# Low parts of the weight blocks by a negated rounding on ScalarE and an accumulating DMA

## Chip, core and metric

The kernel runs on one core of a Trainium2 chip. The metric is the device time of one execution in microseconds (us); the kernel before has a median of 1077.81 us in three runs (1077.65 to 1078.84).

## What is computed

One step of a two-layer decoder trunk, for 1024 prompt tokens and 8 x 4 sample tokens (1056 columns in all, model width 1024), in float32:

```python
# layer 0 (RG-LRU)
u = rmsnorm(x) @ w_in                 # 1024 -> 2 x 1536
xc = causal_conv(u[:1536]);  h = lru_scan(gates(xc), xc)
x = x + (h * silu(u[1536:])) @ w_out
# layer 1 (HGRN2, 8 heads of 128)
q, f, v, gate = split(rmsnorm(x) @ w_in, 4)
o, S = gated_linear_recurrence(silu(q), k(f), v, log_g(f), S0)
x = x + (norm(o) * silu(gate)) @ w_out
y = rmsnorm(x)
```

The outputs are y and the new states of both layers.

## The kernel before

**Split operands.** TensorE multiplies rounded float32 (fp32r). For full precision every operand is held as two blocks, hi = round(x) and lo = x - hi, and a product is three matmuls per 128x128 block (mm3, L241 to L243): hi x hi, hi x lo, lo x hi. For a weight block of 128 partitions and up to 512 columns the steps are these: SP issues the load into a raw buffer (L308), ScalarE rounds raw into hi (L376, L656, L1423, L1648), and GpSimd subtracts, lo = raw - hi (through subtract, L321, or directly, L657 and L1649). In the first 40 us VectorE does some of these subtractions. There are three raw buffers and four slots each for hi and lo in rings (L335); a slot is written again when the matmuls that read it are done. GpSimd also splits activations and does other small work.

**Stages.** Layer 0 runs the input projection (project0, by_chunk) in blocks of 128 outputs over three chunks of 352 columns, with the recurrence (lru) beside it, in four groups; the output projection of three groups is out (residual x loaded from DRAM, added on VectorE at L632 or L696, stored again; nine x buffers, L625), and out_last does the rest with the weights of `load` kept in free tiles. Layer 1 takes its first two heads (HC = 2) with plain products through weights, and the other six with half-size products: seven (L1396) makes two output blocks from seven products of half size instead of eight, after Strassen and Winograd. There split (L1421) rounds and subtracts a raw block or a sum of raw blocks, and combine (L1429) makes those sums on GpSimd, writing over the raw buffers. Five raw buffers serve it; a call of seven has 7 splits and 4 combines, and there are two calls for each of six heads. Between the products lie four bursts per head (burst1 to burst4) with the recurrence: small matmuls on PE and a chain on VectorE (own_gate L1061, scale L1031 and L1040, evacuations L1504 and L1519). The sums of activations that the half-size products read (build, parted_sum: L1363, L321) are made while the first two heads run. Last comes the output projection in two parts; the weights of the second are the eight blocks of `late` (L1640 to L1650).

**Order.** Nothing runs in the order of the program text. Each operation is given to Flow (L39) with its engine, an estimated time, what it reads and writes, a priority and, for a DMA, its size. plan and back (L100, L138) schedule forward and backward several times; each engine then gets its instructions in the order of the best plan. The products of the main chain keep their order on PE. For layer 0 a random search (L165, 3000 tries) also moves operations of the first 60 us. An estimate that changes anywhere can thus change the order everywhere. The warm-up matmuls (L726, 48 calls) fill PE at the start.

The helper that the change adds has these estimates: an activation counts 0.25 + 0.0007 n us on ScalarE, a GpSimd operation with two inputs 0.1 + 0.00245 n, and the new DMA issue 0.93 on GpSimd, with n / 2 KB to move.

Of the kernel before, what the change touches and what calls it, by code (L numbers as in the profile page):

```python
# [14 lines left out]
F32 = mybir.dt.float32  # L15
# [3 lines left out]
AF = mybir.ActivationFunctionType  # L19
ALU = mybir.AluOpType  # L20
# [189 lines left out]
def tile_trunk(ctx: ExitStack, tc: tile.TileContext, xT, prm, hc, w0, wg, wo0, w1, wo1, s_in,  # L210
# [83 lines left out]
    with ExitStack() as l0:  # L294
# [12 lines left out]
        def dma(dst, src, r=(), w=(), prio=5, kb=180, q=Q):  # L307
            fl.add("SP" if q is Q else "ACT", 0.45, lambda: q.dma_start(dst, src), r, w, prio, kb * (1.0 if r else 0.75))  # L308

        def act(n, emit, r, w, prio=5, more=0.0):  # L310
            fl.add("ACT", 0.25 + 0.0007 * n + more, emit, r, w, prio)
# [4 lines left out]
        def pool(n, emit, r, w, prio=5):  # L316
            fl.add("POOL", 0.1 + 0.00245 * n, emit, r, w, prio)
# [45 lines left out]

        def weights(src, n, prio=2, e=G, at=None, q=Q, own=()):

            own = iter(own)
            got = []
            for a in range(0, n, 512):
                m = min(512, n - a)
                raw, *rk = next(own, None) or next(raws)  # L370
                if at:
                    (hi, hk), (lo, lk) = ((o[:, a:a + m], k) for o, k in at)
                else:
                    (hi, hk), (lo, lk) = next(his), next(los)
                dma(raw[:, :m], src[:, a:a + m], (), rk, prio, m / 2, q)
                act(m, lambda hi=hi, raw=raw, m=m: S.copy(hi[:, :m], raw[:, :m]), rk, (hk,), prio)  # L376
                subtract(e, m, lo[:, :m], raw[:, :m], hi[:, :m], (*rk, hk), (lk,), prio)
                got.append((hi, lo, hk, lk))
# [267 lines left out]
        def out_last(src):  # L646
# [3 lines left out]
            def load(m, k, n, hi, hks, lo, lks, kept=()):  # L650
# [5 lines left out]
                act(u, lambda: S.copy(hi, raw[:, :u]), (rk,), (*hks, a), 1)  # L656
                pool(u, lambda: G.tensor_tensor(lo, raw[:, :u], hi.bitcast(F32), op=ALU.subtract), (rk, a), (*lks, b), 1)  # L657
                for i in range(n):
# [266 lines left out]
    with ExitStack() as l1:  # L925
# [470 lines left out]
        def seven(h, a, b, order, at=()):  # L1396
# [24 lines left out]
            def split(p):  # L1421
                (raw, rk), (hi, hk), (lo, lk) = slot[named[p]], next(his), next(los)
                act(512, lambda: S.copy(hi, raw), (rk,), (hk,), 2)  # L1423
                subtract(G, 512, lo, raw, hi, (rk, hk), (lk,), 2)
                parts[p] = hi, lo, (hk, lk)
# [215 lines left out]
        for m in range(KD):  # L1641
# [6 lines left out]
            act(nl, lambda hi=hi, raw=raw: S.copy(hi, raw[:, :nl]), (rk,), (hk,), 1)  # L1648
            pool(nl, lambda hi=hi, lo=lo, raw=raw: G.tensor_tensor(lo, raw[:, :nl], hi.bitcast(F32), op=ALU.subtract), (rk, hk), (lk,), 1)  # L1649
            late.append((hi, lo, (hk, lk)))  # L1650
# [165 lines left out]
```

## Time and profile before

| | |
|---|---|
| median of three runs | 1077.81 us |
| the profiled execution | 1075.47 us |
| its span, first to last instruction | 1073.7 us |
| mean granted TensorE clock | 0.996 |
| instructions on DVE, ACT, POOL | 1535, 1395, 546 |
| DMA issued by SP | 98.67 MB, 28.1% of 16 engines' span |
| DMA issued by GpSimd | none |

PE is TensorE's matmuls, PEld its weight loads, DVE VectorE, ACT ScalarE, POOL GpSimd, and SP issues most DMAs. Lines are those of the kernel before. A group's row has line, engine, operation, out<-in by the program's names, shapes and count, then busy us and mean ns of one, then the engine's idle time before it and what ended it. A row of waits has engine and line of what waited, what it waited for, then the total in us, the number of times and the longest. A row of a timeline has start, length, and the instruction. The page's row of a DMA issue has the name of the tile, count, KB each and the median us from issue to landing. wlo and whi are the low and rounded parts of weights.

### The profile page before, as it was taken

To read this page: it belongs to the slowest core of one execution; us is meant where nothing else is said; L and a number is where in the kernel's file an instruction comes from. 1 tells how busy PE (TensorE), PEld (TensorE's weight loads), DVE (VectorE), ACT (ScalarE), POOL (GpSimd) and SP (SyncE) were. 2 spreads that over 40 slices of the span, in tenths; PEclk is the share of its full clock that TensorE was granted. 3 is DMA by queue.
4 is the path that set the end of the run, shared out by engine and by line. 5 is a ranking of instruction groups with operands and counts; after the bars stand their busy time and mean duration, and the time that the engine had idled before them with its cause. 6 is when DMAs were issued, how large, how long until landed. Compare 5 with 4: busy or idle time off the path is not lost.

```text
span 1073.7 us, 25345 instructions
## 1 busy us (share of the span) xinstructions
PE 1053.0 (98%) x9972; PEld 1024.5 (95%) x9972; DVE 808.2 (75%) x1535; ACT 611.1 (57%) x1395; POOL 558.0 (52%) x546
## 2 busy tenths in 40 slices
PE   9999999999999999999999998999999999999997
PEld 9999999999999999999998997999999999989996
DVE  8999996887997787283999997767768585774446
ACT  7578656867665964243364563747474655752323
POOL 3425353353543547455574854656566665541545
PEclk9999999999999999999999999999999999999998
DMA  9101112124832775240110121212121212354204
GB/s 302 59 27 43 56 49 71 58 61 126 271 104 66 222 252 176 103 131 34 60 51 24 49 92 43 100 43 91 35 92 41 91 44 80 116 169 160 85 1 162
DMA packets 70119, 103.05 MB, mean 96 GB/s; under 512 B 9200, under 2 KB 51184, under 8 KB 70000
## 3 DMA queue, kind: packets, MB, share of 16 engines
q1 hardware_dynamic: 67696, 98.67, 28.1%
q10 hardware_dynamic: 2304, 2.77, 0.8%
q8 instruction: 78, 1.28, 0.5%
q14 instruction: 41, 0.34, 0.1%
HBM read 71.05 MB, written 25.49 MB: 90 GB/s over the span
## 4 chain that ended last, share of the span: by engine, by line
PE 82%; DVE 14%; issue 1%; DMA 1%; ACT 1%; POOL 0%; SPq 0%; POOLq 0%; ACTq 0%; DVEq 0%
PE mm L241 23%; PE mm L242 22%; PE mm L243 22%; PE hg L1049 2%; DVE R L1363 1%; DVE R L1031 1%; PE hg L1266 1%; PE hg L565 1%; DVE tmp L1363 1%; PE hg L1158 1%; DVE a L1232 1%; PE hg L1268 1%; DVE sg L1031 1%; PE hg L241 1%; PE hg L242 1%
## 5 line engine op out<-in xcount | busy, mean ns | idle before, releaser
L241 PE MATMUL mm<-xh,whi 128*128 128x352 f32 (+1 forms) x1143 | 359.3, 314 | 7.2 <-DVE sg L1504 4.5
L242 PE MATMUL mm<-xl,whi 128*128 128x352 f32 (+1 forms) x1143 | 353.2, 309 | 0.0
L243 PE MATMUL mm<-xh,wlo 128*128 128x352 f32 (+1 forms) x1143 | 353.2, 309 | 0.0
L321 POOL TENSOR_TENSOR wlo<-wraw,whi 128x512 fp32r<-128x512 f32 (+2 forms) x131 | 175.9, 1351 | 168.7 <-ACT whi L376 83.6
L241 PEld LDWEIGHTS mm<-xh,whi 128*128 128x128 f32 x1143 | 214.7, 188 | 10.5 <-DVE sg L1504 6.0
L242 PEld LDWEIGHTS mm<-xl,whi 128*128 128x128 f32 x1143 | 215.0, 188 | 1.6 <-DVE xl L321 0.2
L243 PEld LDWEIGHTS mm<-xh,wlo 128*128 128x128 f32 x1143 | 214.9, 188 | 0.0
L497 DVE SCALAR_TENSOR_TENSOR k<-xb,prm_sb,k 128x352 f32<-128x352 f32 (+2 forms) x144 | 90.1, 637 | 10.9 <-ACT k L494 6.1
L241 PE MATMUL mm<-t,whi 128*128 128x264 f32 (+1 forms) x306 | 89.5, 293 | 0.0
L242 PE MATMUL mm<-t,whi 128*128 128x264 f32 (+1 forms) x306 | 87.7, 287 | 0.0
L243 PE MATMUL mm<-t,wlo 128*128 128x264 f32 (+1 forms) x306 | 87.5, 286 | 0.0
L580 POOL TENSOR_TENSOR k<-X 128x352 f32<-128x352 f32 x36 | 44.9, 1256 | 47.8 <-DVE R L581 38.6
L321 POOL TENSOR_TENSOR wlo<-R,whi 128x512 fp32r<-128x512 f32 x33 | 49.9, 1511 | 32.8 <-ACT whi L1423 28.9
L376 ACT CAST whi<-wraw 128x512 fp32r<-128x512 f32 (+2 forms) x83 | 46.0, 574 | 28.5 <-PE mm L242 16.9
L241 PEld LDWEIGHTS mm<-t,whi 128*128 128x128 f32 x306 | 57.6, 188 | 0.7 <-ACT k L1481 0.5
L1504 DVE TENSOR_TENSOR k<-mm,k 128x264 f32<-128x264 f32 x62 | 26.5, 430 | 41.5 <-PE mm L243 41.4
L243 PEld LDWEIGHTS mm<-t,wlo 128*128 128x128 f32 x306 | 57.7, 188 | 0.0
L242 PEld LDWEIGHTS mm<-t,whi 128*128 128x128 f32 x306 | 57.6, 188 | 0.0
L1031 DVE TENSOR_TENSOR R<-R,sg 128x512 f32<-128x512 f32 (+1 forms) x48 | 50.4, 1050 | 0.1
L241 PE MATMUL mm<-yh,whi 128*128 128x352 f32 x153 | 49.9, 326 | 0.0
L243 PE MATMUL mm<-yh,wlo 128*128 128x352 f32 x153 | 49.4, 323 | 0.0
L242 PE MATMUL mm<-yl,whi 128*128 128x352 f32 x153 | 49.4, 323 | 0.0
(415 smaller groups left out, 2684.6 us busy)
## 6 DMA issues: line engine op xcount, KB each, us to landing
wraw<-in_w_dram SPq DMA_DIRECT2D x91, 256.0 KB, 2.6
wraw<-in_wo_dram SPq DMA_DIRECT2D x34, 192.0 KB, 2.5
si<-in_s_in_dram SPq DMA_DIRECT2D x8, 512.0 KB, 4.2
out_ss_out_dram<-si SPq DMA_DIRECT2D x8, 512.0 KB, 2.6
sg<-x1b SPq DMA_DIRECT2D x21, 176.0 KB, 2.8
x<-sg SPq DMA_DIRECT2D x21, 176.0 KB, 1.8
R<-in_w_dram SPq DMA_DIRECT2D x14, 256.0 KB, 2.5
R<-td SPq DMA_DIRECT2D x72, 44.0 KB, 2.0
```

The costliest lines, as they stand in the source:

```text
L241: T.matmul(out, wh, xh, start=first, stop=False, skip_group_check=chained)
L242: T.matmul(out, wh, xl, start=False, stop=False, skip_group_check=chained)
L243: T.matmul(out, wl, xh, start=False, stop=last, skip_group_check=chained)
L321: emit = lambda: e.tensor_tensor(b, x, a.bitcast(F32), op=ALU.subtract)
L376: act(m, lambda hi=hi, raw=raw, m=m: S.copy(hi[:, :m], raw[:, :m]), rk, (hk,), prio)
L497: dve(u, lambda src=src, dst=dst, sh=sh, k=k: V.scalar_tensor_tensor(dst, sh(src, k), pc("cw", 12 * k + m), dst, op0=ALU.mult, op1=ALU.add ...
L565: fl.add("PE", 0.62, lambda ps=ps, i=i, c=c: T.matmul(ps[:96, :CH], gs[:, i, :], ST[:96, chunk(c)], start=True, stop=True), (("gs",), *((" ...
L580: pool(CH, lambda x=x, a=a, b=b: G.tensor_tensor(x, a.bitcast(F32), b.bitcast(F32), op=ALU.add), (ak, bk), (xk,), 3)
L1031: dve(n // 2, lambda sv=sv, dv=dv, s=s, f=f: V.tensor_tensor(dv[:, :, s, :], sv[:, :, s, :], f, op=ALU.mult), (*sk, *gk), dk if i == o els ...
L1049: T.matmul(ps[32 * j:32 * j + 32, n * w:n * w + w], B[:, o:o + 32], q(slice(o, o + 32)), start=True, stop=True, tile_position=(0, 32 * j))
L1363: dve(n, lambda: V.tensor_tensor(o, a, b, op=op), r, (w,), prio, True)
L1504: dve(QT, lambda: V.tensor_tensor(o[0], z[0], u[0], op=ALU.add), (z[1], u[1]), (o[1],), 0)
```

## The change

A new helper `low` makes the low part without hi: ScalarE writes -round(raw) into lo, and a DMA issued by GpSimd adds raw to it (an accumulating DMA). So lo = raw - round(raw) as before. It is used for every weight block that GpSimd subtracted through weights (the default e=G becomes e=None), for the blocks of split in seven, and for the eight late blocks: 176 blocks by the counts of the code. The 18 blocks of `load` in out_last go from GpSimd to VectorE. Blocks for which the call names an engine (the first six of layer 0), the gate weights of lru, and all activations stay. The DMA reads raw and reads and writes lo, so combine and the next load into that raw buffer wait for its landing. The added lines shift later line numbers by 5 to 8.

```diff
+        def low(n, dst, src, r, w, prio=5):
+
+            act(n, lambda: S.activation(dst, src, AF.Copy, scale=-1.0), r, w, prio)
+            fl.add("POOL", 0.93, lambda: G.dma_start(dst.bitcast(F32), src, accum_op=ALU.add), (*r, *w), w, prio, n / 2)
+
...
-        def weights(src, n, prio=2, e=G, at=None, q=Q, own=()):
+        def weights(src, n, prio=2, e=None, at=None, q=Q, own=()):
...
-                subtract(e, m, lo[:, :m], raw[:, :m], hi[:, :m], (*rk, hk), (lk,), prio)
+                if e is None:
+                    low(m, lo[:, :m], raw[:, :m], rk, (lk,), prio)
+                else:
+                    subtract(e, m, lo[:, :m], raw[:, :m], hi[:, :m], (*rk, hk), (lk,), prio)
...
-                pool(u, lambda: G.tensor_tensor(lo, raw[:, :u], hi.bitcast(F32), op=ALU.subtract), (rk, a), (*lks, b), 1)
+                subtract(V, u, lo, raw[:, :u], hi, (rk, a), (*lks, b), 1)
...
-                subtract(G, 512, lo, raw, hi, (rk, hk), (lk,), 2)
+                low(512, lo, raw, (rk,), (lk,), 2)
...
-            pool(nl, lambda hi=hi, lo=lo, raw=raw: G.tensor_tensor(lo, raw[:, :nl], hi.bitcast(F32), op=ALU.subtract), (rk, hk), (lk,), 1)
+            low(nl, lo, raw[:, :nl], (rk,), (lk,), 1)
```

## Prediction

> **What bounds the kernel now.** I read the page first: busy time, then the engines of the chain that ended last.
>
> ```profile
> span 1073.7 us, 25345 instructions
> ...
> PE 1053.0 (98%) x9972; PEld 1024.5 (95%) x9972; DVE 808.2 (75%) x1535; ACT 611.1 (57%) x1395; POOL 558.0 (52%) x546
> ...
> PE 82%; DVE 14%; issue 1%; DMA 1%; ACT 1%; POOL 0%; SPq 0%; POOLq 0%; ACTq 0%; DVEq 0%
> ```
>
> TensorE is idle for 1073.7 - 1053.0 = 20.7 us, and the change leaves every matmul as it is. So it can gain 20.7 us at most, whatever it takes off GpSimd. Next, a table by stage says where the idle time lies, and the view of waits of PE says for whom.
>
> ```profile
> 0.00:50.00 50.00, 47.83 (x317) 46.73 (x318) 44.56 (x99) 32.27 (x67) 18.63 (x27) 1.00 0.58 193
> 50.00:500.00 450.00, 450.00 (x2770) 443.32 (x2769) 353.85 (x632) 286.04 (x561) 208.97 (x234) 1.00 0.35 109
> ...
> 565.00:570.00 5.00, 2.98 (x82) 2.60 (x81) 4.93 (x5) 3.86 (x9) 3.75 (x3) 1.00 0.07 16
> ...
> 645.00:655.00 10.00, 6.12 (x55) 5.24 (x55) 9.72 (x19) 1.99 (x4) 5.12 (x6) 1.00 0.03 9
> ...
> 660.00:935.00 275.00, 271.89 (x3880) 262.08 (x3881) 189.93 (x376) 165.41 (x438) 171.66 (x139) 1.00 0.21 72
> ...
> 1050.00:1073.70 23.70, 16.94 (x127) 15.68 (x125) 14.33 (x35) 7.97 (x18) 11.74 (x14) 0.83 0.52 184
> ```
>
> ```profile
> PE mm L241 <- DVE sg L1504: 4.5, 7, 0.8
> PE mm L241 <- DVE attns L1056: 2.7, 1, 2.7
> PE hg L1049 <- DVE R L1061: 2.0, 1, 2.0
> PE mm L241 <- ACT xh L1590: 1.4, 1, 1.4
> ```
>
> After the length, the columns are busy time of PE, PEld, DVE, ACT, POOL, then granted clock, DMA share and GB/s. From 50 to 500 us PE never stops: nothing can be won there, only lost. The tail (23.7 - 16.9 = 6.8 us) and the start (2.2 us) hold no block that the change touches. What is left is 2.0 us at 565-570 and 3.9 us at 645-655, both with DVE busy over 97% of the time, 3.1 us spread over 660-935, and the wait on L1590 (1.4 us).
>
> **The change, part by part.** It removes 194 subtractions from GpSimd. In 176 of them ScalarE writes the negated block and a DMA issued by GpSimd adds the raw block to it; 18 (L657) go to VectorE. The two largest shapes (count | busy us, mean ns), the main one of L657 (shortest, median, longest ns, first to last start), the rounding on ScalarE, and the stage of L657:
>
> ```profile
> L321 POOL TENSOR_TENSOR wlo<-wraw,whi 128x512 fp32r<-128x512 f32 x109 | 151.5, 1395 | 155.3 <-ACT whi L376 70.1 <-ACT whi L1423 53.1 <-DMA sg<-x 11.6
> L321 POOL TENSOR_TENSOR wlo<-R,whi 128x512 fp32r<-128x512 f32 x33 | 49.9, 1511 | 32.8 <-ACT whi L1423 28.9 <-PE hg L1049 3.9
> ```
>
> ```profile
> L657 POOL TENSOR_TENSOR X<-wraw,X x8: 1022/1255/1387, 400.2 to 414.8; 128x384 fp32r<-128x384 f32 x8
> ```
>
> ```profile
> L376 ACT CAST whi<-wraw 128x512 fp32r<-128x512 f32 x61 | 36.9, 618 | 28.4 <-PE mm L242 16.9 <-DMA wraw<-in_w_dram 5.1 <-DMA R<-td 3.7
> ```
>
> ```profile
> 400.00:450.00 50.00, 50.00 (x316) 50.00 (x315) 26.78 (x50) 18.08 (x41) 29.56 (x34) 1.00 0.45 144
> ```
>
> ScalarE: the negation has the shape of the rounding beside it, so 142 x 0.618 + 34 smaller ones of at most 0.618 = at most 109 us, ending near 720 of 1074 us. It lies beside matmuls, so the path pays 0. VectorE gets 18 subtractions, each bounded above by GpSimd's longest, 1.387: at most 25 us, most of them from 400 us on, where VectorE has 23.2 of 50 us free and PE is full; 0 again. If ScalarE or VectorE had no room there, each 1 us of theirs would cost 1 us.
>
> GpSimd: no DMA issue of its own is in the trace. Its cost lies between nearly nothing and the 1.395 us that it replaces; I take 1.0 (the planner in the code writes 0.93). GpSimd's own time is on the path with 0%, so its saving is worth 0 in itself.
>
> SP: a weight load waits until its raw buffer is released, now by the landing instead of by the subtraction, 0.62 + 1.0 + 2.6 - 1.4 = 2.8 us later and more. From 250 to 400 us SP waited for that already:
>
> ```profile
> SPq L308 <- POOL wlo L321: 22.8, 10, 10.1
> ```
>
> PE was full there all the same, so I take 0; without that cover it is part of the first rival. The 2.6 is a load's time to landing, shown with that rival.
>
> What is on the path is what the subtraction does to VectorE. The timeline at 642 us, VectorE then GpSimd, and that VectorE line's shortest, median and longest:
>
> ```profile
> 642.15 4.46 DVE L1519 SCALAR_TENSOR_TENSOR sg<-sg,k 128x264 f32<-128x264 f32 x1
> ```
>
> ```profile
> 642.56 1.27 POOL L321 TENSOR_TENSOR wlo<-wraw,whi 128x512 fp32r<-128x512 f32 x1
> 643.79 1.30 POOL L321 TENSOR_TENSOR wlo<-R,whi 128x512 fp32r<-128x512 f32 x1
> 645.05 1.27 POOL L1431 TENSOR_TENSOR wraw<-R,wraw 128x512 f32<-128x512 f32 x1
> ```
>
> ```profile
> L1519 DVE SCALAR_TENSOR_TENSOR sg<-sg,k x24: 419/424/4464, 634.9 to 946.5; 128x264 f32<-128x264 f32 x24
> ```
>
> ```profile
> L321 POOL TENSOR_TENSOR wlo<-wraw,whi 128x512 fp32r<-128x512 f32 x8 | 12.5, 1572 | 1.3 <-ACT whi L376 1.3
> ```
>
> A VectorE operation of 0.42 us takes 4.46, and it ends at 646.6, just after GpSimd's unbroken run passes from one L1431 to the next. Two of the run are low parts: without them it ends 1.27 + 1.30 = 2.57 us sooner. Right behind it PE stands still. I take 3.0 of the 3.9 us at 645-655 (2.57 plus a little from the other subtractions since 600). The last row is GpSimd between 510.9 and 567.6 us, the VectorE chain that PE waits for at 567: 8 subtractions, 12.5 us. They can hold VectorE up by 0 to 12.5 us; a sixth of that closes the 2.0 us gap, so I take 2.0. Of the waits on L1504, L1590 and L321 I take nothing. Something else is late next after two such gaps close, and for it I put back 1.0 us, an estimate between 0 and the 5.0.
>
> The Trainium skill, SBUF — State Buffer, "Who interferes with whom", has this as a lock: a VectorE instruction with two SBUF inputs and a GpSimd instruction that reads SBUF exclude each other for the whole instruction. The 4.46 us agrees. By it a DMA's descriptor writing, which reads no SBUF, leaves such VectorE work alone; no run yet shows that.
>
> Sum: 0 + 0 - 3.0 - 2.0 + 1.0 = **-4.0 us**, so the profiled execution's 1075.47 us (its span plus 1.8) becomes 1071.5. The three timed runs have a median of 1077.81, 2.34 above that execution; carried over, 1073.8.
>
> **Rivals.** First, **the DMA fills up**. Two stretches are full of loads and stores already:
>
> ```profile
> 276.00:300.00 24.00, 24.00 (x152) 24.00 (x151) 21.98 (x33) 15.33 (x28) 11.90 (x10) 1.00 0.92 283
> 368.00:396.00 28.00, 28.00 (x175) 27.76 (x174) 25.09 (x39) 20.93 (x33) 17.26 (x12) 1.00 0.90 282
> ```
>
> ```profile
> q1 hardware_dynamic: 67696, 98.67, 28.1%
> ...
> wraw<-in_w_dram SPq DMA_DIRECT2D x91, 256.0 KB, 2.6
> ```
>
> ```profile
> x1a<-k SPq DMA_DIRECT2D x9, 176.0 KB, 3.3
> wraw<-in_w_dram SPq DMA_DIRECT2D x6, 256.0 KB, 4.4
> xo<-in_xT_dram SPq DMA_DIRECT2D x6, 176.0 KB, 3.8
> ```
>
> Of low parts these stretches hold, first the one, then the other:
>
> ```profile
> L321 POOL TENSOR_TENSOR wlo<-wraw,whi 128x512 fp32r<-128x512 f32 x4 | 5.7, 1436 | 8.4 <-ACT whi L376 7.0 <-DMA wraw<-in_w_dram 1.3
> L321 POOL TENSOR_TENSOR wlo<-wraw,whi 128x384 fp32r<-128x384 f32 x3 | 4.6, 1565 | 1.6 <-ACT whi L376 1.6
> ```
>
> ```profile
> L321 POOL TENSOR_TENSOR wlo<-wraw,whi 128x512 fp32r<-128x512 f32 x4 | 6.6, 1641 | 5.8 <-ACT whi L376 5.8
> ...
> L321 POOL TENSOR_TENSOR wlo<-wraw,whi 128x384 fp32r<-128x384 f32 x2 | 3.6, 1810 | 0.0
> ```
>
> 28.1% of 1073.7 us for 98.67 MB is 3.06 us per MB, so a block of 256 KB occupies all engines for 0.80 us if an accumulation costs what a copy does, and I allow twice that. With 4 blocks of 256 KB and 3 and 2 of 192, 5.0 to 10.0 and 4.4 to 8.8 us are added where only 1.9 (8% of 24) and 2.8 are free: a backlog of up to 8.1 and 6.0 us. The residual x has nine buffers; one product there is 9 matmuls 0.16 us apart (593.72 to 593.88 below), so a buffer comes round in 13.0 us, of which load and store (the last rows, median us to landing from 250 to 300) take 3.8 + 3.3 and the add some 0.5 (an estimate, from L1519's 0.42 at 264 columns): 5.4 us to spare. PE loses 0 to 2.7 + 0.6 = 3.3 us, and with the gain kept the result is 1073.8 to 1077.1. The Trainium skill, DMA: Bandwidth & Descriptors, "Rules for kernel authors", says that an accumulating DMA reads its destination and writes it later; a third pass speaks for the upper end, and nothing here shows it.
>
> ```profile
> 593.72 0.32 PE L241 MATMUL mm<-xh,whi 128*128 128x352 f32 x1
> 593.88 0.32 PE L242 MATMUL mm<-xl,whi 128*128 128x352 f32 x1
> ```
>
> ```profile
> 694.38 1.03 PE hg L1049 x64
> ...
> 752.16 1.03 PE hg L1049 x64
> ```
>
> Second, **the gain is swallowed**: the next operation of the same VectorE chain, or the new order of everything that the planner makes, ends as late. Then it is 1077.8, no change. The same follows if GpSimd's descriptor writing holds VectorE up as the subtraction did.
>
> Third, the other side: **in the half-size products the low part comes late**. A head takes 752.16 - 694.38 = 57.8 us and has 14 such products, 4.1 us each. With four slots a block must be ready three products after its slot comes free: 12.4 us. Now the way is 0.62 + 1.4 = 2.0 us. Then it is 0.62 + 0.62 + 1.0 + landing, 2.6 to 5.2 (a load's 2.6 and twice it; 4.4 where the DMA is full), 4.8 to 7.4 us. But combine (L1431) overwrites raw blocks, so in GpSimd's order it waits for those DMAs to land, and the low part queued behind it waits too: another landing and two combinations of 1.4, 10.2 to 15.4 us in all. It decides from 12.4 on. If one product in each of the 12 calls of seven is late by 1 to 3 us, the loss is 12 to 36 us; by 1.5 it is 18, and the result 1073.8 + 18 = 1091.8. For it: those waits stand in the changed order of GpSimd. Against it: this worst queueing need not meet the tightest slot, and SP and GpSimd both run far ahead of PE here (GpSimd 172 of 275 us busy).
>
> **How the numbers follow.** Forecast 0.45, DMA stretches 0.12, swallowed 0.15, late low parts 0.28. A measurement of this kernel tells about 0.2%, 2.2 us, from no change: faster is under 1075.7, slower over 1080.0. The forecast is faster; the first rival ends on either side of 1075.7, mostly within, and with the swallowed gain makes 0.27 for the same; late low parts are slower, 0.28. Predicted: 1073.8. The range starts at 1069.5, the forecast with the other waits on VectorE gained too, and reaches 1088, about half of the third rival's cases, so that some 0.15 to 0.2 is left out.
>
> **What would show it.** Right: PE idle under 1.5 us in each of 565-570 and 645-655 (or where these products then lie), VectorE's busy time down by tens of us, the longest L1519 near 1 us, and 50 to 500 us still full. The DMA rival: PE waits on the adds of L632 near 280 or 380 us, DMA share at 1.0. The third: PE waiting for wlo or for a DMA of wlo between 590 and 940 us, and a head that takes more than 57.8 us. I am wrong if the landing of such a DMA takes well over 5 us, or GpSimd is held for over 1.4 us by each issue.

## Result and profile after

The changed kernel takes 1082.22 us (median of five executions, 1080.83 to 1086.73), the kernel before 1077.65 us on the same chip: ratio 1.0048, 95% interval 1.0025 to 1.0072. The change makes it slower by about 4.6 us, where 4 us faster was forecast. The profiled execution took 1080.83 us.

The page of the changed kernel, its first rows and the engines of the chain that ended last; lines are now those of the changed kernel, 5 to 8 higher:

```profile
span 1079.0 us, 25709 instructions
## 1 busy us (share of the span) xinstructions
PE 1059.0 (98%) x9972; PEld 1031.4 (96%) x9972; DVE 715.1 (66%) x1553; ACT 696.4 (65%) x1571; POOL 448.0 (42%) x528
...
PE 88%; DVE 5%; DMA 4%; issue 1%; ACT 1%; POOL 0%; SPq 0%; ACTq 0%; POOLq 0%; DVEq 0%
```

The change did what it says: VectorE is busy 93 us less and GpSimd 110 us less, ScalarE 85 us more. Yet the span is 5.3 us longer, and DMA has entered the chain with 4%. PE's busy time has grown by 6 us for the same matmuls, and a part of this is its clock, shown below. Now the DMA queues and two of the issues of the new kind on the same page:

```profile
q1 hardware_dynamic: 67696, 98.67, 29.4%
q0 software_dynamic: 25344, 43.00, 23.9%
...
wlo<-wraw POOLq DMA_DIRECT2D x109, 256.0 KB, 4.0
...
wlo<-R POOLq DMA_DIRECT2D x33, 256.0 KB, 4.2
```

The accumulations move 43.00 MB in 23.9% of 1079.0 us, 6.0 us of all engines per MB; the loads and stores take 29.4% for 98.67 MB, 3.2 us per MB. An accumulation costs 1.87 times a copy, 1.57 us per 256 KB, near the upper bound of the prediction (1.60). This agrees with the rule of the Trainium skill (DMA: Bandwidth & Descriptors, "Rules for kernel authors") that it reads its destination besides. The load of these two queues together went from 28.1% to 53.3%.

The stages that the prediction looked at, in the changed kernel (the tail is cut at the new end):

```profile
0.00:50.00 50.00, 46.11 (x293) 45.40 (x294) 41.17 (x91) 29.73 (x62) 18.96 (x26) 0.97 0.61 192
50.00:500.00 450.00, 446.32 (x2733) 439.00 (x2732) 316.54 (x642) 312.61 (x613) 147.22 (x209) 1.00 0.54 140
565.00:570.00 5.00, 5.00 (x33) 5.00 (x32) 4.89 (x9) 3.91 (x9) 2.75 (x3) 1.00 0.32 110
645.00:655.00 10.00, 10.00 (x214) 9.50 (x213) 4.94 (x13) 6.55 (x17) 5.92 (x6) 1.00 0.57 116
660.00:935.00 275.00, 275.00 (x3826) 266.03 (x3825) 161.22 (x385) 199.69 (x509) 140.32 (x138) 1.00 0.62 136
1050.00:1079.00 29.00, 21.28 (x154) 20.01 (x152) 17.55 (x42) 9.97 (x21) 14.60 (x17) 0.93 0.43 150
```

Both gaps that were to close are closed (5.00 of 5.00, 10.00 of 10.00), and 660 to 935 has no idle time left, against 3.1 us before. What is new stands above them: 50 to 500 us, full before, now has 3.7 us of idle time, and the start has 1.7 us more. The waits of PE in the changed kernel say for what (total us, times, longest):

```profile
PE mm L243 <- DMA wlo<-wraw: 3.8, 2, 2.6
PE mm L241 <- DVE sg L533: 2.9, 1, 2.9
PE mm L241 <- ACT xh L1598: 2.3, 1, 2.3
PE mm L241 <- DVE k L640: 1.1, 1, 1.1
```

They lie at 404 us (and 610), 34, 948 and 276 us. Finer windows of the changed kernel around them, and then two of the same windows of the kernel before:

```profile
30.00:35.00 5.00, 2.15 (x12) 1.86 (x11) 4.69 (x11) 3.43 (x8) 3.78 (x3) 0.87 0.25 76
35.00:40.00 5.00, 5.00 (x26) 4.79 (x26) 4.12 (x11) 2.54 (x7) 1.15 (x2) 0.79 0.71 213
260.00:276.00 16.00, 14.96 (x87) 13.64 (x85) 7.22 (x18) 12.75 (x21) 3.86 (x6) 1.00 0.96 252
380.00:406.00 26.00, 23.41 (x144) 22.87 (x143) 14.41 (x27) 19.47 (x33) 5.25 (x6) 1.00 1.03 291
...
950.00:955.00 5.00, 5.00 (x16) 4.36 (x17) 1.18 (x3) 3.34 (x8) 2.29 (x3) 0.50 0.90 254
```

```profile
260.00:276.00 16.00, 16.00 (x94) 15.03 (x93) 10.49 (x20) 15.42 (x24) 8.96 (x7) 1.00 0.64 199
380.00:406.00 26.00, 26.00 (x165) 26.00 (x164) 23.34 (x37) 16.02 (x31) 11.63 (x11) 1.00 0.73 232
```

The DMA share, last but one, went from 0.64 to 0.96 and from 0.73 to 1.03: the stretches around out() are full. And where PE stood still at 34 and 948 us its granted clock then fell, to 0.50 at 950 to 955 us: PE is "busy" there and does half the work, 2.5 us lost besides the wait.

To compare all kernels by stage, one number is used from here on: **PE's lost time**. For each two matmuls that follow one another, take the time from start to start and subtract the median for that shape in the kernel before; add up by stage. It holds waits, slower clock and slower pace alike, of the one profiled execution, and that is not always a typical one: the profile of the kernel before took 1075.47 us, below all its timed executions, those of half again and of planner's size doubled 1072.31 and 1088.75 us, 3.4 and 5.7 us above their medians. The sum also holds what lies behind 1050 us, 1.1 to 2.7 us. (The layer borders are near 490 us; 500 to 590 us are mostly the first two heads of layer 1, 590 to 925 the half-size products, 925 to 1050 the change-over to the output projection.) Medians of several executions and their ratio to the kernel before on the same chip stand beside it; from chip to chip the kernel before has 1077.3 to 1078.7 us, so compare kernels by their ratios.

| kernel | median us | ratio (95%) | 0-50 | 50-250 | 250-500 | 500-590 | 590-925 | 925-1050 | sum |
|---|---|---|---|---|---|---|---|---|---|
| before | 1077.65 | 1 | 3.7 | 2.1 | 3.2 | 6.4 | 26.9 | 8.0 | 51.7 |
| after | 1082.22 | 1.0048 (1.0025-1.0072) | 7.6 | 3.4 | 7.8 | 3.8 | 21.5 | 10.8 | 56.3 |
| layer 1 alone | 1071.53 | 0.9954 (0.9941-0.9967) | 3.9 | 2.1 | 3.2 | 3.8 | 25.2 | 9.2 | 48.6 |
| layer 0 alone | 1086.97 | 1.0091 (1.0078-1.0104) | 5.0 | 3.4 | 9.0 | 4.5 | 28.3 | 10.7 | 62.6 |
| split alone | 1075.92 | 0.9994 (0.9983-1.0004) | 3.7 | 2.1 | 3.2 | 9.9 | 22.2 | 9.9 | 52.1 |
| without out | 1077.37 | 0.9996 (0.9987-1.0004) | 4.2 | 3.5 | 5.5 | 4.5 | 24.3 | 9.4 | 53.4 |
| planner's size doubled | 1083.01 | 1.0051 (1.0038-1.0064) | 5.1 | 3.0 | 14.6 | 3.9 | 23.5 | 12.1 | 64.9 |
| other seed | 1081.15 | 1.0025 (1.0012-1.0038) | 6.2 | 3.2 | 6.9 | 4.4 | 25.1 | 10.5 | 58.1 |
| without by_chunk | 1080.93 | 1.0024 (1.0013-1.0035) | 5.0 | 3.5 | 3.7 | 4.8 | 23.4 | 10.2 | 52.0 |
| without both | 1076.34 | 0.9988 (0.9977-1.0000) | 4.3 | 3.5 | 3.9 | 4.5 | 23.7 | 10.0 | 51.1 |
| load on GpSimd | 1084.32 | 1.0059 (1.0045-1.0073) | 4.5 | 3.6 | 11.4 | 3.8 | 23.5 | 9.6 | 58.2 |
| layer 1 + copies | 1085.13 | 1.0065 (1.0052-1.0077) | 6.6 | 3.6 | 10.8 | 3.6 | 25.2 | 9.9 | 61.6 |
| layer 1 + DRAM copies | 1086.23 | 1.0073 (1.0058-1.0087) | 5.4 | 3.7 | 11.7 | 3.7 | 24.3 | 11.5 | 62.3 |
| subtract again | 1089.00 | 1.0109 (1.0096-1.0122) | 4.0 | 2.1 | 3.2 | 9.2 | 32.1 | 12.8 | 65.1 |
| fill | 1103.16 | 1.0236 (1.0223-1.0249) | 3.6 | 2.1 | 3.2 | 4.5 | 50.6 | 13.1 | 78.8 |
| half again | 1068.88 | 0.9917 (0.9897-0.9937) | 4.6 | 2.1 | 3.2 | 3.8 | 24.0 | 8.5 | 48.0 |
| half fill | 1069.09 | 0.9919 (0.9905-0.9932) | 3.6 | 2.1 | 3.2 | 4.0 | 20.3 | 9.6 | 44.3 |
| split and first weights | 1070.59 | 0.9928 (0.9910-0.9946) | 4.3 | 2.1 | 3.2 | 3.8 | 23.9 | 8.6 | 47.4 |
| same order, subtract | 1089.77 | 1.0106 (1.0092-1.0120) | 3.8 | 2.1 | 3.2 | 8.8 | 35.8 | 10.6 | 66.1 |
| other hand-over | 1078.53 | 1.0007 (0.9998-1.0016) | 4.0 | 2.1 | 3.2 | 10.1 | 24.2 | 10.8 | 56.0 |

After against before: +3.9, +1.3 and +4.6 in layer 0, -2.6 and -5.4 in layer 1, +2.8 at the change-over: 4.6 in sum, of the 5.3 us of span. **Theory**: the accumulations fill the DMA in layer 0 (the prediction's first rival, larger), and the gain of layer 1 is as forecast. **Rivals**: every stage is a little slower and the gain is a lucky order; or low parts are late by their own way through the DMA, without any lack of bandwidth.

### The profile page after: what moved, and what is told of

The parts are those of the page before. It is cut to its first block, busy times and chain, and to the rows that moved or that the text cites. A ratio compares the mean times of both kernels' runs of the same rounds, so it can differ in the third digit from the quotient of the medians.

```text
span 1079.0 us, 25709 instructions
## 1 busy us (share of the span) xinstructions
PE 1059.0 (98%) x9972; PEld 1031.4 (96%) x9972; DVE 715.1 (66%) x1553; ACT 696.4 (65%) x1571; POOL 448.0 (42%) x528
## 3 DMA queue, kind: packets, MB, share of 16 engines
q1 hardware_dynamic: 67696, 98.67, 29.4%
q0 software_dynamic: 25344, 43.00, 23.9%
## 4 chain that ended last, share of the span: by engine, by line
PE 88%; DVE 5%; DMA 4%; issue 1%; ACT 1%; POOL 0%; SPq 0%; ACTq 0%; POOLq 0%; DVEq 0%
PE mm L241 24%; PE mm L243 24%; PE mm L242 24%; PE hg L1057 2%; DMA wlo<-wraw 1%; PE hg L1166 1%; DVE k L505 1%; PE hg L1274 1%; PE hg L1220 1%; PE hg L1276 1%; DMA wraw<-in_wo_dram 1%; PE hg L573 1%; PE hg L241 1%; PE hg L243 1%; PE hg L242 1%
## 5 line engine op out<-in xcount | busy, mean ns | idle before, releaser
L313 POOL DMA_DIRECT2D wlo<-wraw x131 | 116.8, 923 | 174.7 <-ACT wlo L312 134.6
L312 ACT ACTIVATE wlo<-wraw 128x512 fp32r<-128x512 f32 (+2 forms) x131 | 77.6, 602 | 44.4 <-PE mm L243 35.3
L505 DVE SCALAR_TENSOR_TENSOR k<-xb,prm_sb,k 128x352 f32<-128x352 f32 (+2 forms) x144 | 79.3, 559 | 16.4 <-ACT k L502 8.2
L588 POOL TENSOR_TENSOR k<-X 128x352 f32<-128x352 f32 x36 | 41.6, 1158 | 67.6 <-DVE R L589 62.3
L1512 DVE TENSOR_TENSOR k<-mm,k 128x264 f32<-128x264 f32 x62 | 26.3, 429 | 52.6 <-PE mm L243 52.3
L313 POOL DMA_DIRECT2D wlo<-R x33 | 30.0, 908 | 49.3 <-ACT wlo L312 46.4
```

Source lines behind the costliest of these rows:

```text
L312: act(n, lambda: S.activation(dst, src, AF.Copy, scale=-1.0), r, w, prio)
L313: fl.add("POOL", 0.93, lambda: G.dma_start(dst.bitcast(F32), src, accum_op=ALU.add), (*r, *w), w, prio, n / 2)
L505: dve(u, lambda src=src, dst=dst, sh=sh, k=k: V.scalar_tensor_tensor(dst, sh(src, k), pc("cw", 12 * k + m), dst, op0=ALU.mult, op1=ALU.add ...
L588: pool(CH, lambda x=x, a=a, b=b: G.tensor_tensor(x, a.bitcast(F32), b.bitcast(F32), op=ALU.add), (ak, bk), (xk,), 3)
L1512: dve(QT, lambda: V.tensor_tensor(o[0], z[0], u[0], op=ALU.add), (z[1], u[1]), (o[1],), 0)
```

## Experiments

### One layer at a time

The two layers are planned one after the other, so that one of them can be changed with the other's order as it was. For layer 1 alone, layer 0 gets back its subtractions (so in all five calls of weights there, and in load); layer 0 alone is the complement.

```diff
-                w = weights(src, 1024)
+                w = weights(src, 1024, e=G)
...
-                subtract(V, u, lo, raw[:, :u], hi, (rk, a), (*lks, b), 1)
+                subtract(G, u, lo, raw[:, :u], hi, (rk, a), (*lks, b), 1)
```

> Low parts by the accumulating DMA in layer 1 alone (its weights, split and late); layer 0 subtracts on GpSimd as before. Theory A (stage by stage): what was lost lies in layer 0 (stalls and pace of PE up to 500 us: 3.9 + 1.3 + 4.6 = 9.8 us), the half-size stage gained 8.0 us, and the change-over at 925 to 1050 us lost 2.8 us. Then this kernel is 8.0 - 2.8 = 5.2 us faster than before: 1072.5 us, ratio 0.995. Theory B (DMA and clock over the whole run: the accumulating DMA makes every stage a little slower and the gain in the half-size stage was a lucky order): within 2 us of before.

> The other half: the change in layer 0 alone (its weights through the DMA, the 18 blocks of load on VectorE); layer 1 as before. Theory A: 9.8 us slower than before, 1087.5 us, ratio 1.009, with PE stalls near 34, 276 and 404 us as in the changed kernel. Theory B: half of the net loss, 2 to 3 us slower, ratio 1.002.

Layer 1 alone: 1071.53 us, ratio 0.9954, a gain of 5.0 +- 1.4 us. Layer 0 alone: ratio 1.0091, a loss of 9.8 +- 1.4 us. Their sum is the changed kernel (-0.46 + 0.91 = +0.45% against +0.48%), and the rival of a loss spread over the run falls. In the first 500 us the two halves repeat the stages of the kernels that they are taken from, up to a scatter at the start and, in layer 0 alone, 1.2 us more from 250 to 500 us, where the clock fell (0.57 from 402 to 406 us) behind the same wait of 2.6 us that it didn't fall behind in the changed kernel.

### Which blocks of layer 0

Each of these is the changed kernel with some low parts on GpSimd again: the 24 blocks of out(), those of by_chunk, or both; and the 18 of load.

```diff
-                w = weights(wo0[m][:, 384 * g:384 * g + 384], 384)
+                w = weights(wo0[m][:, 384 * g:384 * g + 384], 384, e=G)
...
-            ws = [weights(src, 1024) for src, _ in items]
+            ws = [weights(src, 1024, e=G) for src, _ in items]
```

> The changed kernel, but the 24 low parts of out()'s weights (192 KB each, the blocks that fall into the stretches full of loads and stores) subtracted on GpSimd again. If these DMAs cause the loss from 250 to 475 us (the first rival of the prediction), this is 4.6 us faster than the changed kernel: 1077.6 us, ratio 1.000 to before. If the loss there comes from the 18 blocks of load on VectorE or from other blocks, it stays at the changed kernel's 1082 us, ratio 1.004.

> The changed kernel, but the low parts of by_chunk's blocks (the ones that PE waits for at 404 us) subtracted on GpSimd again. Theory L (the way through the DMA makes just these low parts late: issue 0.9 and landing 5.6 to 6.7 us in a full stretch against 1.4 for a subtraction): the stall at 404 us is gone or under 0.5 us and the time is 2.7 us shorter, 1079.5 us, ratio 1.002; the stall near 276 us (1.2 us, on a residual) stays. Theory T (the other accumulations fill the DMA, so the raw block comes late too): PE still stalls 1.5 us or more near 400 us, and the time stays within 1.5 us of 1082.

> The changed kernel, but out()'s and by_chunk's low parts, all that fall into the stretches of layer 0 with the DMA full, subtracted on GpSimd; the other low parts of layer 0 still go through the DMA. If only the place matters (full stretches), 50 to 500 us cost what they cost before (5.3 us of stalls and pace) and the time is that with the change in layer 1 alone, 1071.5 us, plus up to 2 us of the start: 1071 to 1074 us, ratio 0.994 to 0.9965. If the accumulating DMAs cost PE something wherever they are, it stays near the kernel without out()'s alone, 1077 us.

> The changed kernel, but the 18 subtractions of load stay on GpSimd. The prediction took them at 0 on VectorE: then 1082 us as the changed kernel, ratio 1.004, but for up to 2 us by which a new order shifts it. If VectorE lacked the room, 2 to 4 us faster, with the gain in 250 to 500 us.

Without out()'s 24 blocks the time is that of before (1077.37); the loss from 250 to 500 us halves, and a start shorter by 3.4 us comes with it. The blocks that PE waits for at 404 us belong to by_chunk. The view of tile wlo of the changed kernel, 392 to 406 us, shows their way (shortest, median, longest ns, then first and last start):

```profile
L313 POOL DMA_DIRECT2D wlo<-wraw x2: 869/869/869, 398.5 to 399.6; - x2
...
  PE mm L243: 2.6, 1
...
DMA to landing us min/median/max: 5.6/6.2/6.7
```

Issued at 398.5 and 399.6, they land up to 6.7 us later in a full stretch. Without by_chunk's accumulations the profiled execution has no wait of PE from 250 to 500 us:

```profile
250.00:500.00 250.00, 250.00 (x1538) 246.45 (x1537) 170.61 (x328) 158.78 (x310) 88.39 (x113) 1.00 0.65 179
```

But this execution was its fastest (1076.69 us, the median is 1080.93), and the intervals of its ratio and the changed kernel's (1.0024 and 1.0048) overlap, so the window bears out only that these low parts can be late, not that they alone cost the 4.6 us. With both left out, the stage is back to 3.9 us, and the median at 1076.34, about that of before (ratio 0.9977 to 1.0000); still some 3.7 us above layer 1 alone by the ratios (0.9988 and 0.9954), where 0 to 2 was expected. 2.5 us of that stand in the table (start, 50 to 250 and 250 to 500 us); the rest is open. The 18 subtractions on VectorE cost nothing: without them it is no faster.

### Planning and the start

Twice the size in the planner's books (n for n / 2) and another seed of the random search.

```diff
-            fl.add("POOL", 0.93, lambda: G.dma_start(dst.bitcast(F32), src, accum_op=ALU.add), (*r, *w), w, prio, n / 2)
+            fl.add("POOL", 0.93, lambda: G.dma_start(dst.bitcast(F32), src, accum_op=ALU.add), (*r, *w), w, prio, n)
```

```diff
-        rng = Random(1)
+        rng = Random(2)
```

> The changed kernel, but the planner counts each accumulating DMA with twice its size (n KB instead of n / 2 for n columns), near the 1.5 us of all DMA engines that the trace shows for 256 KB. Theory L (lateness: the order is planned for DMAs that land too early by the plan): blocks are loaded earlier, the stalls near 276, 404 and 610 us go (1.2 + 2.7 + 1.4), and the time is 1082.2 - 5.3 = 1077 us, ratio 0.9995. Theory T (traffic: the stretches of layer 0 hold more bytes than the DMA engines move, in any order): the stalls move and stay as large, 1081 to 1083 us, ratio 1.0035 to 1.005.

> The changed kernel with another seed (2 for 1) of the random search over the first 60 us; the order behind that and all of layer 1 stay. If the 3.9 us lost in the first 50 us are luck of that search, this start differs by some us: between 1078.3 (loss gone) and 1083 us. If accumulating DMAs crowd the start whatever its order, PE still loses over 7 us in 0 to 50 us and the time stays at 1082 us.

Counting the transfers higher doesn't help: the median is at the upper end of what the theory of traffic had, and in the profile, this kernel's slowest execution, the stall that ends at 405 us is longer than ever. PE's waits from 250 to 620 us of it:

```profile
PE mm L243 <- DMA wlo<-wraw: 8.6, 2, 5.7
```

The other seed lies between the two theories: 0 to 50 us cost 6.2 instead of 7.6 us, and its executions reach from 1076.72 to 1084.96. Over all profiles, kernels with layer 0 as before lose 3.6 to 4.6 us there, kernels with a changed layer 0 lose 4.2 to 7.6. So the changed start is worse on the whole, with much scatter between orders and between executions of one order (after and layer 0 alone: 7.6 and 5.0). Traffic of the accumulations can't be the reason, since in the changed kernel the first of them is issued at 83.6 us; here are most of them (shortest, median, longest ns, first to last start):

```profile
L313 POOL DMA_DIRECT2D wlo<-wraw x131: 850/880/1244, 83.6 to 1013.1; - x131
```

### Traffic without late low parts

On the kernel with layer 1 alone, GpSimd also issues two plain copies for each block of layer 0 that the change had moved, to DRAM that nothing reads. In the second kernel they go from DRAM to DRAM and hold no raw buffer. The low parts come from GpSimd's subtraction.

```diff
                 subtract(e, m, lo[:, :m], raw[:, :m], hi[:, :m], (*rk, hk), (lk,), prio)
+                    if e is G and at is None and fl.until:
+                        for o in (next(turn), next(turn)):
+                            fl.add("POOL", 0.93, lambda o=o, raw=raw, m=m: G.dma_start(o[:, :m], raw[:, :m]), rk, (("junk", id(o)),), prio, m / 4)
```

```diff
+                            fl.add("POOL", 0.93, lambda o=o, a=a, m=m: G.dma_start(o[:, :m], src[:, a:a + m]), (hk,), (("junk", id(o)),), prio, m / 4)
```

> The kernel with the change in layer 1 alone (1071.5 us), and on top GpSimd issues, for each block of layer 0 that the change moved to the DMA, two plain copies of the raw block to DRAM that nothing reads; the low parts are still subtracted on GpSimd, so they do not wait for any of it. The traffic is that of the accumulations or a little more (2 x 0.8 us of all DMA engines for 256 KB against 1.5), and raw buffers are held until it lands. Theory T (traffic and held buffers): PE loses 4 to 5 us more between 50 and 500 us, with waits on residual adds near 280 and 390 us: 1075.5 to 1077 us, ratio 0.9985. Theory L (late low parts): 1071 to 1073 us, ratio 0.9945 to 0.996.

> The kernel with the change in layer 1 alone, and for each block of layer 0 that the change moved two copies of the same weights from DRAM to DRAM, issued by GpSimd: traffic without any hold on raw buffers or low parts. Traffic alone: PE loses 4 to 7 us more between 50 and 500 us than without, with waits on residual adds, 1076 to 1084 us, ratio 0.999 to 1.006. Held raw buffers: 1071 to 1073 us, ratio 0.9945 to 0.996.

Both bring the loss back in full, and more than the theory of traffic had said: 10.8 and 11.7 us from 250 to 500 us where layer 1 alone has 3.2. GpSimd's queue from 50 to 500 us, in the changed kernel, with copies and with DRAM copies (packets, MB, share of 16 engines):

```profile
q0 software_dynamic: 8064, 13.64, 18.1%
```

```profile
q0 software_dynamic: 8448, 27.27, 16.3%
```

```profile
q0 software_dynamic: 8448, 27.27, 18.7%
```

The three put about the same load on the DMA engines. PE's waits from 50 to 500 us with the DRAM copies, and a wait of VectorE there:

```profile
PE mm L243 <- DVE k L645: 3.9, 3, 1.4
PE hg L578 <- ACT td L580: 0.6, 1, 0.6
PE hg L243 <- ACT R L574: 0.4, 1, 0.4
```

```profile
DVE k L645 <- DMA k<-in_xT_dram: 2.6, 1, 2.6
```

L645 is the residual add (L632 before). PE waits for it at 270, 277 and 374 us. At 277 VectorE had waited for x from DRAM (the row above), as the first rival said; at 374 it had waited 2.7 us for another load, a block of the recurrence, ahead of the add; at 270 for no load. With a lower clock behind the wait at 277 us (0.93 on average from 276 to 300 us, some 1.7 us) the waits make up 6.7 of the 8.5 us that were added. **Traffic is enough**; neither a late low part nor a held raw buffer is needed. Two things came with the copies that no run separates from their traffic: GpSimd issues them (it is busy 259 instead of 209 us from 50 to 500 us), and layer 0 has another order. But none of PE's waits there is for GpSimd, and without both, in another order too, the stage lost only 3.9 us. These kernels lose more than the changed one, so low parts aren't free of lateness either, but that isn't where it begins. From 50 to 250 us, where no wait is new, every kernel with this traffic loses 3.0 to 3.7 us and every one without it 2.1; why matmuls follow each other less closely there wasn't tested.

### What layer 1 gained

With split alone, the weights of the first two heads are subtracted on GpSimd as before, and so are layer 1's output weights (e=G there, and subtract for low in late):

> Only the 84 low parts of split (half-size products) by the DMA; everything else as before. Theory A: the gain of the half-size stage, 8.0 us, without the lost 2.8 us at the change-over if these come from the eight late blocks: 1069.7 us, ratio 0.9925; 1072.5 if the change-over is lost all the same. Theory B: within 2 us of before. Were low parts late in the half-size products (the third rival of the prediction), PE would wait on DMAs of wlo between 590 and 940 us.

The half-size stage gains 4.7 us, but 500 to 590 us lose 3.5, and with the change-over the sum is nothing, where 5 to 8 us of gain were expected. PE's waits from 500 to 590 us with split alone; the kernel with layer 1 alone has none:

```profile
PE hg L1057 <- DVE sg L1039: 2.4, 1, 2.4
PE hg L1111 <- DVE a L1039: 0.9, 1, 0.9
```

To see whether it is VectorE, held up by GpSimd, layer 1 alone gets work for GpSimd that nobody waits for: it subtracts each block again (on 64 partitions, 2 x 256 columns, into a spare tile), or writes memsets in place of that. Then the same with half the dose.

```diff
+        def again(m, raw, hi, r):
+            for a in range(0, m, 256):
+                q = slice(a, min(m, a + 256))
+                pool(q.stop - a, lambda q=q, n=q.stop - a: G.tensor_tensor(scr[0][:, :n], raw[64:, q], hi[64:, q].bitcast(F32), op=ALU.subtract), r, (("scr",),), 6)
```

```diff
-                ... G.tensor_tensor(scr[0][:, :n], raw[64:, q], hi[64:, q].bitcast(F32), op=ALU.subtract) ...
+                ... [G.memset(scr[0][:, :u], 0.0) for u in (n, n, n // 2)] ...
```

> The kernel with the change in layer 1 alone (1071.5 us), and on top GpSimd subtracts each block of layer 1's first weights, of split and of layer 1's output weights again, in two halves of 256 columns on 64 partitions, into a tile that nothing reads: the low parts still come from the DMA, GpSimd is busy as before. Theory A (what layer 1 gained is VectorE, held up by a GpSimd that reads SBUF): the gain goes, 1075.5 to 1077.5 us, ratio 0.9985 to 1.000, and the longest L1519-type operations of VectorE are over 2 us again. Theory C (the gain is the other order, or an earlier low part): stays at 1071 to 1073 us, ratio 0.995.

> As the kernel that subtracts again, with memsets (256, 256 and 128 columns) in the place of each half subtraction: GpSimd is planned as busy as there and busy for about as long, but reads no SBUF for it. Theory A: the gain stays, 1071 to 1073 us, ratio 0.995, and VectorE's operations are as short as without the memsets. If GpSimd's time as such (its queue) set the pace, this is as slow as the kernel that subtracts again: 1075.5 to 1077.5 us.

> The kernel with the change in layer 1 alone (1071.5 us), with GpSimd subtracting the first 256 columns of each of those blocks again into a tile that nothing reads (0.9 us each, half of the dose of the kernel that subtracted all again). Theory A (layer 1's gain is VectorE, held up by a GpSimd that reads SBUF): VectorE is busy about 25 to 30 us longer than without, 775 to 780 us, and the time is 2 to 5 us longer, 1073.5 to 1077 us, ratio 0.996 to 0.9995. Theory C (order or earlier low parts): 1071 to 1072.5 us, ratio 0.994 to 0.9955.

> The same with memsets (256, 256 and 128 columns, 0.9 us together) in the place of each of those subtractions. Theory A: VectorE stays at 750 to 755 us busy and the time at 1071 to 1073 us, ratio 0.994 to 0.996, below the kernel that subtracts again. If GpSimd's queue is what counts: as slow as that kernel or slower.

The busy time of VectorE answers clearly. The page's row of layer 1 alone, then of half again and of half fill:

```profile
PE 1053.2 (98%) x9972; PEld 1026.3 (96%) x9972; DVE 751.8 (70%) x1535; ACT 664.3 (62%) x1511; POOL 504.9 (47%) x546
```

```profile
PE 1054.4 (98%) x9972; PEld 1027.5 (96%) x9972; DVE 781.6 (73%) x1535; ACT 664.0 (62%) x1511; POOL 593.2 (55%) x654
```

```profile
PE 1052.4 (99%) x9972; PEld 1026.4 (96%) x9972; DVE 750.1 (70%) x1535; ACT 664.6 (62%) x1511; POOL 593.2 (56%) x870
```

The same instructions of VectorE take 30 us longer beside half subtractions, and no longer beside memsets that keep GpSimd as busy. The row of the operation that the prediction showed (L1519 before), by groups, in these two:

```profile
L1538 DVE SCALAR_TENSOR_TENSOR sg<-sg,k 128x264 f32<-128x264 f32 x24 | 20.9, 879 | 1.9 <-ACT sg L1537 1.8
```

```profile
L1538 DVE SCALAR_TENSOR_TENSOR sg<-sg,k 128x264 f32<-128x264 f32 x24 | 10.2, 429 | 5.2 <-ACT sg L1537 4.7
```

Mean 879 against 429 ns. A GpSimd that only writes SBUF, or issues DMAs, doesn't hold such VectorE work up; one that reads it does. This agrees with the Trainium skill (SBUF — State Buffer, "Who interferes with whom"). For the issues the changed kernel shows it: 32 operations of this line (L1527 there) lie beside an issue and beside no subtraction or sum of GpSimd, and the longest takes 453 ns. But the time of the kernel does not follow: half again takes 1068.88 us, half fill 1069.09 on the same chip, both with a lower ratio than layer 1 alone. So 30 us of VectorE cost nothing that these runs can tell when the planner may place them (each ratio is known to 1.4 to 2.2 us), and the forecast of 2 to 5 us was wrong. With the full dose GpSimd's own queue got in the way, at least in the kernel with memsets; a wait of VectorE there (500 to 950 us) shows a small operation of GpSimd that came late behind them:

```profile
DVE kt L1315 <- POOL rst L1312: 26.9, 7, 6.8
```

So that pair couldn't tell the theories apart. The last two kernels ask for the order. The first keeps every engine's order of layer 1 alone, the negation too, and only subtracts on GpSimd where it had issued the DMA; where ScalarE's rounding comes later in that order, it subtracts the block that the slot held before, so it doesn't compute the reference. The second is the kernel before with another order of layer 1.

```diff
-            ... G.dma_start(dst.bitcast(F32), src, accum_op=ALU.add) ...
+            ... G.tensor_tensor(dst, src, hi.bitcast(F32), op=ALU.subtract) ...
```

```diff
         fl = Flow(side=0.4)
+        fl.HOP = 0.22
```

> The kernel with the change in layer 1 alone (1071.5 us), every engine in the same order, ScalarE's negation included; only, where GpSimd issued an accumulating DMA it now subtracts raw - hi itself, so that the negated block is overwritten without use. Theory C (order): the time stays at 1069 to 1073 us, ratio 0.992 to 0.996. Theory A (the subtraction itself, by holding up VectorE and lying longer in GpSimd's queue): back to before or worse, 1075.5 to 1080 us, ratio 0.998 to 1.002, with VectorE 50 us busier than with the DMAs.

> The kernel before, but the planner of layer 1 counts 0.22 us for a hand-over between engines instead of 0.20: nothing is computed or moved in another way, the order of layer 1 alone is another. If a new order is worth as much as the change (theory C), the time moves by 2 us or more either way, outside 1075.5 to 1080 us or near its ends; if orders are worth less than 1 us, it stays at 1077 to 1079 us, ratio 0.999 to 1.001.

Another order alone: ratio 1.0007, no change that can be told, though the stages shift by up to 3.7 us against one another. The same order with subtractions: 1089.77 us, by the ratios some 16 us above layer 1 alone, more than either theory had said. Its page and its waits of PE from 500 to 960 us:

```profile
PE 1058.5 (97%) x9972; PEld 1029.8 (95%) x9972; DVE 810.9 (74%) x1535; ACT 663.7 (61%) x1511; POOL 558.2 (51%) x546
```

```profile
PE mm L241 <- ACT k L1489: 7.3, 7, 1.2
PE mm L241 <- DVE sg L1512: 4.5, 6, 1.4
PE mm L241 <- DVE k L1512: 2.6, 1, 2.6
PE hg L1057 <- DVE sg L1039: 2.2, 1, 2.2
```

VectorE is busy 59 us longer, and PE waits for its evacuations (L1512) and, longest in sum, for ScalarE's (L1489): from 706 to 884 us 1.2 us in each of four heads. VectorE stands behind these too: at 704, 763 and 822 us a copy of ScalarE ahead of L1489 has to wait for its chain (L1039). One of the operations of that chain, in layer 1 alone and then here (the kernel before has the same median, 1798 ns):

```profile
L1039 DVE TENSOR_TENSOR a<-a,ST x8: 691/707/708, 526.0 to 923.1; 128x528 f32<-128x528 f32 x8
```

```profile
L1039 DVE TENSOR_TENSOR a<-a,ST x8: 691/1798/1803, 526.7 to 940.9; 128x528 f32<-128x528 f32 x8
```

So layer 1's gain comes from the subtraction that is no longer there, and another order by itself is worth nothing; but the order decides how much of the gain is felt, some 16 us in this one and 5 us against the order that was planned for subtractions. How it divides between a VectorE held up and a longer queue on GpSimd isn't settled.

### The change-over

Split and the first weights through the DMA, the output weights of layer 1 subtracted:

```diff
-                ws2[m] = weights(wo1[m][:, :128 * K1], 128 * K1, at=at_)
+                ws2[m] = weights(wo1[m][:, :128 * K1], 128 * K1, e=G, at=at_)
...
-            low(nl, lo, raw[:, :nl], (rk,), (lk,), 1)
+            subtract(G, nl, lo, raw[:, :nl], hi, (rk, hk), (lk,), 1)
```

> Low parts by the DMA for split and for layer 1's first weights; layer 1's output weights (WO1 and late), whose loads and low parts run near 925 to 965 us, subtract on GpSimd as before, and so does layer 0. If the accumulations there fill the DMA and make the change-over dearer (it cost 8.0 us before, 9.2 to 10.8 with them): back to 8 us, 1070.3 us, ratio 0.9935. If it is the order: 9 to 10 us as in the kernel with split alone, 1071 to 1072.5 us.

925 to 960 us of layer 1 alone, then of this kernel:

```profile
925.00:960.00 35.00, 31.59 (x469) 29.71 (x468) 21.77 (x57) 21.05 (x67) 14.73 (x17) 0.95 0.87 229
```

```profile
925.00:960.00 35.00, 32.01 (x471) 30.23 (x470) 23.95 (x59) 19.72 (x62) 16.75 (x18) 0.95 0.58 172
```

The DMA is far from full there now (0.58 for 0.87), and the stage costs 8.6 instead of 9.2 us: between the two theories, and a difference smaller than that between layer 1 alone and the changed kernel (9.2 and 10.8), which have the same layer 1. What makes the change-over dearer than in the profile of the kernel before is not the change. Here is the same window of the kernel before, of layer 0 alone and of other hand-over:

```profile
925.00:960.00 35.00, 32.49 (x548) 29.99 (x547) 25.84 (x57) 21.12 (x65) 16.95 (x18) 1.00 0.55 173
```

```profile
925.00:960.00 35.00, 31.89 (x423) 30.42 (x423) 26.84 (x56) 19.87 (x50) 17.19 (x18) 0.93 0.48 145
```

```profile
925.00:960.00 35.00, 31.57 (x413) 30.32 (x412) 23.34 (x50) 17.95 (x50) 15.15 (x16) 0.90 0.52 154
```

Layer 0 alone runs layer 1 as before, in the same order on VectorE, ScalarE, GpSimd and SP, and other hand-over has no accumulating DMA at all; yet they lose 10.7 and 10.8 us at the change-over, as much as the changed kernel. PE waits 2.9 and 3.4 us there for the xh of ScalarE, and the granted clock falls behind it. It falls at the change-over in every profile but that of the kernel before, where this wait is 1.4 us. So it is that one execution that was cheap there. At 1070.59 us, ratio 0.9928, this kernel beats both the one before and the changed one, as layer 1 alone does.

## Why the prediction was wrong

Its sum was about right for layer 1 and had nothing for layer 0. The sum -3.0 - 2.0 + 1.0 = -4.0 us came from the gaps at 565 and 645 us, both layer 1; that layer alone gave -5.0 +- 1.4. Layer 0 gave +9.8 +- 1.4 where every term was 0.

- **The step that failed**: "PE was full there all the same, so I take 0", for 250 to 400 us and SP's waits. A full PE says that there is no idle time to win; it doesn't say how much the supply can slip. The DMA had 8 to 10% free from 276 to 300 and from 368 to 396 us, which the prediction itself had quoted. With the accumulations the full stretches begin earlier and end later: its share was 0.96 from 260 to 276 us and 1.03 from 380 to 406 us, the residual adds and by_chunk's blocks came late, and the profile lost 4.6 us from 250 to 500 us where the sum had 0.
- **First rival, "the DMA fills up"**: right in mechanism (L640's add at 276 us; traffic without late low parts suffices) and in the price of a block (1.57 us of 0.80 to 1.60), too low in size and chance: 0 to 3.3 us and 0.12, against 4.6 us from 250 to 500 us, and a kept gain. It counted two stretches by the positions before the change and only the residual's buffers, not the weight blocks loaded in the same stretch (2.6 us of PE's waits are for their wlo, at 404 us).
- **"The start holds no block that the change touches"**: true of the blocks, wrong of the time. The search over the first 60 us sees different operations behind them, and PE waited 2.9 us for VectorE in the changed kernel, with a lower clock after it, and 1.7 us in layer 0 alone: the start cost 3.9 and 1.3 us more. That the search is the reason was not shown; the other seed still lost 2.5 us more than before.
- **The gap at 645-655 us, -3.0**: it closed, and 590 to 925 us gained 5.4 in this profile (2.6 as a mean over the eight other kernels with the same layer 1). The longest L1527 on the same tiles (L1519 before, 4464 ns) fell as forecast:

```profile
L1527 DVE SCALAR_TENSOR_TENSOR sg<-sg,k x24: 418/424/435, 641.6 to 948.0; 128x264 f32<-128x264 f32 x24
```

- **The gap at 565-570 us, -2.0**: closed, -2.6 for its stage. Not all of it is the subtractions': in layer 0 alone, with layer 1 as before, this wait is 0.7 instead of 2.0 us. With that stage's subtractions back and split's away, 3.3 us of waits on VectorE return there.
- **+1.0 put back**: the 2.8 us at the change-over (2.5 us of them are five microseconds at a clock of 0.50) are not this term, since layer 0 alone pays 2.7 there with layer 1 as before. What came late next in layer 1 was not found.
- **Rival three, late low parts in the half-size products**: came once, a wait of 1.2 us for wlo at 610 us, in place of 12 to 36 us; no other up to the end. A head takes 56.8 us (756.66 to 813.42, first matmul of the same burst) where it took 57.8.
- **Zero terms that held**: VectorE's 18 subtractions, ScalarE's 85 us (taken: at most 109), GpSimd's issue of 0.9 us where 1.0 was taken, a median landing of 4.0 to 4.2 us in 2.6 to 5.2. "Swallowed by a new order" didn't happen to layer 1 as a whole; with split alone it did.

## What to carry to other kernels

Where an engine is full in a stage, ask what supplies it and how much that has to spare there: work moved from a compute engine to the DMA is paid for in and beside the stretches where the DMA was already at 0.9, not on the average. Price an accumulating DMA between SBUF tiles at about two copies, as here. Try such a change by stage: here it was worth -5 us in one layer and +10 in the other, and taking it in one layer alone beat both whole kernels.

## What the runs showed of the hardware besides

- An accumulating DMA from SBUF to SBUF, 128 x 512 float32: 0.9 us of GpSimd for the issue, 4.0 to 4.2 us to landing as a median, 6.7 in a full stretch, 6.0 us of all DMA engines per MB against 3.2 for loads and stores.
- The granted clock of TensorE fell to 0.50 for 3.4 and 6.8 us behind two waits of PE, of 2.9 us (34 us) and 2.3 us (948 us), and didn't behind waits of 2.6 us (404 us) and, in the kernel before, 2.7 us (650 us). In layer 0 alone it did fall behind the same two waits (2.6 us, 2.7 us). The length of a wait alone doesn't decide. The Trainium skill (TensorE: Matmul & The Clock Gate, "HAM oscillation — how this bites in real kernels") warns of gaps over about 3.4 us; here shorter ones were enough.
- Two kernels with work that nobody needs (half again, half fill) have the lowest ratios, 0.9917 and 0.9919, against 0.9954 of layer 1 alone. Split and first weights, 0.9928, can't be told from them. No run here says why.
